# A second pair of block products taken one level further apart in two of sixteen groups

## Chip, core and metric

The kernel runs on one core of one Trainium2 chip. The metric is the device time of one execution in microseconds (us). The engines are named as in the profile: PE (TensorE matmuls), PEld (its weight loads), DVE (VectorE), ACT (ScalarE), POOL (GpSimd, which here only issues DMAs) and SP (SyncE, which issues the stores).

## What is computed

```python
m, k, n = 4096, 4096, 4096          # a, b: standard normal, float32
def reference(a, b):
    x = np.matmul(a, b)
    return 0.5 * x * (1 + np.tanh(np.sqrt(2 / np.pi) * (x + 0.044715 * x**3)))
```

The output is float32. The operands are rounded to float16 when they are loaded, and the sums are kept in float32.

## The kernel before

**Seven products instead of eight.** A and B are cut into quadrants of 2048 x 2048, and the four quadrants of the output are put together from seven products of sums of quadrants (Strassen's method). `PRODUCTS` lists them as (name, chain, A operand, B operand); `("11", "12", -1)` means A11 - A12, and a bare `"22"` means the quadrant itself:

```python
    ("M3", "Y", "11", ("12", "22", 1)),
    ("M5", "X", ("11", "12", -1), "22"),
    ("M7", "X", ("12", "22", -1), ("21", "22", 1)),
    ("M1", "X", ("11", "22", -1), ("11", "22", -1)),
    ("M4", "X", "22", ("21", "11", 1)),
    ("M2", "Y", ("22", "21", -1), "11"),
    ("M6", "Y", ("21", "11", -1), ("11", "12", 1)),
```

**Groups and steps.** The output quadrants are worked off in 16 groups, 0 to 15. A group is a block of 512 rows and 512 columns in each quadrant: (mb, nb), with mb changing every four groups. A group does its seven products in the order above (the last group has the order `LAST`). A product has a depth of 2048 and takes 4 steps (q = 0 to 3) of 16 matmuls, each 128 x 128 weights times 128 x 512. Products of one chain, X or Y, add up in the same four PSUM banks; `bank` (L390) gives a group four banks for X and four for Y, which swap roles from group to group. `settle` takes a product out of PSUM when its last step has run through bank i, by ACT copies (L513), DVE additions (L549), the gelu on ACT (L540) and the store by SP (L543).

**Split products.** In the groups of `SPLIT_GROUPS` (11, 13, 14, 15) the pair M3 and M5 goes one level further: each is itself done as seven products, "1" to "7", on quarters of its operands. `PAIR` is their order: "2", "1", "3" of M3, the same of M5, then "4", "5" of both, then "7", "6" of both. A small step is 16 matmuls of 128 x 256 (L483); in "2" the first matmul of each of two banks is 512 wide, to clear the whole bank. The parts are joined in PSUM and in a tile `join` by ACT copies (L501, L506) and DVE additions (L498). If an A operand is a sum of quadrants, the sum is first built in two tiles `aD` (four DVE instructions), and five of the seven small products take a further sum of its quarters.

**Where operands come from.** In the groups 0 to 5 the B sums are built on DVE (L365) and stored to DRAM, in units `k_M...` of 1 MB (two for each product). From group 6 on B is no longer in SBUF: the units are fetched (L760, `fetch`, a POOL DMA) into a ring of eight tiles of 1 MB. For a split pair the seven units `k_split` are fetched, two small operands in each. They are built in the groups 6, 7, 9 and 10 (the `maker` of each nb) by `make_split`: the quarters are added by DVE (L763, into one of three buffers `bS`) and stored by SP (L337); the two raw quarters, "2" and "5", of each product are copied out of the ring tile into `k_split` by SP alone.

**The order is planned by hand.** `steps` is the list of all steps of PE. Before the kernel is written out, a loop over the groups from 6 on hangs tasks on step numbers: an operand sum of A two steps ahead of its use (`AHEAD`), or six for split steps (`SPLIT_AHEAD`); a fetch at most twelve steps ahead (`FETCH_AHEAD`) and not before its ring tile is free; `ring_place` gives out the eight tiles in turn. `before` holds what comes from outside this plan: loads of A into the two `stage` tiles (L206, POOL), their transposition (L181, DVE) and the row checks (L228, ACT). The tasks give each engine's queue its order; an engine then runs each instruction as soon as its own waits are over, also ahead of the step that it is hung on. All queues are strictly in order, POOL's and SP's too, so one waiting fetch holds back all that are behind it.

A second path, `general_path`, is in the program for inputs whose range the checks reject; it does not run here.

Of the kernel before, what the change touches and what calls it, by code (L numbers as in the profile page):

```python
# [7 lines left out]
F32 = mybir.dt.float32  # L8
F16 = mybir.dt.float16
# [29 lines left out]

LAST = [PRODUCTS[k] for k in (0, 1, 3, 4, 5, 6, 2)]  # L40
NP = len(PRODUCTS)
QPH = 4
# [12 lines left out]

PAIR = [(s, p) for ps in ("213", "45", "76") for s in (0, 1) for p in ps]
SPLIT_AHEAD = 6
FETCH_AHEAD = 12
SPLIT_GROUPS = (11, 13, 14, 15)
CHECK_GROUP = 9  # L60
# [60 lines left out]
def half_path(  # L121
# [199 lines left out]
    def product(gi, s):  # L321
        return (LAST if gi == len(groups) - 1 else PRODUCTS)[s]

# [64 lines left out]
    post = {}  # L388

    def bank(gi, chain, i):  # L390
        par = (gi + (chain == "Y")) % 2
        t = psum_pool.tile([P, NC], F32, name=f"acc{chain}", tag=f"bank{par}{i}")
        banks[chain, i] = t
        return t
# [58 lines left out]
    def multiply(gi, s, q):  # L453
        name, chain = product(gi, s)[:2]
        first = q == 0 and name in ("M3", "M5")
        sa, sb = sums.pop((gi, s, q))
        for i in range(RT):
            acc = bank(gi, chain, i) if first else banks[chain, i]
            products(acc, sa, sb, i, first, q == QPH - 1)
            if q == QPH - 1:  # L460
                settle(gi, name, i)
# [7 lines left out]
    def multiply_split(gi, s, p):  # L469
# [6 lines left out]
        for r in range(RT // 2):  # L476
# [12 lines left out]
            if p in "76":  # L489
                settle(gi, name, i)  # L490
        if p in "24":
            joins[chain, p] = pool.tile([P, NC], F32, name="join", tag="x1", bufs=RT)
        for r in range(RT // 2):
            def join(p):
                return joins[chain, p][:, r * NC // 2 : (r + 1) * NC // 2]

            def joined(out, x, y, op):
                nc.vector.tensor_tensor(out=out, in0=x, in1=y, op=op)  # L498

            if p == "2":  # L500
                nc.scalar.copy(out=join("2"), in_=region(chain, "21", r))  # L501
            elif p == "3":
                joined(join("2"), region(chain, "12", r), join("2"), ALU.subtract)
                joined(join("2"), region(chain, "11", r), join("2"), ALU.add)
            elif p == "4":
                nc.scalar.copy(out=region(chain, "22", r), in_=join("2"))  # L506
                joined(join("4"), region(chain, "21", r), join("2"), ALU.add)
            elif p == "5":
                joined(region(chain, "11", r), join("4"), region(chain, "12", r), ALU.subtract)

# [40 lines left out]
    def settle(gi, name, i):  # L551

        X, Y = banks.get(("X", i)), banks.get(("Y", i))
        end = gi == len(groups) - 1
        if name == "M5":
            if end:
# [26 lines left out]
        elif name == "M6":  # L583
# [3 lines left out]
            waiting.append((gi, i, 1, 1, y, y))  # L587


    steps = [(0, -1, n) for n in range(N_PLAIN)]  # L590
    steps += [(0, s, q) for s in range(NP) for q in range(QPH // 2, QPH)]
    for gi in range(1, len(groups)):
        if gi in SPLIT_GROUPS:
            steps += [(gi, s, p) for s, p in PAIR]
        else:
            steps += [(gi, s, q) for s in (0, 1) for q in range(QPH)]
        steps += [(gi, s, q) for s in range(2, NP) for q in range(QPH)]
    position = {step: n for n, step in enumerate(steps)}
# [3 lines left out]
    def step_number(gi, s, q):  # L602
        gi, s = gi + s // NP, s % NP
        return position.get((gi, s, q), first_step[gi] + s * len(SPLIT) + 2 * q)

# [66 lines left out]
    def stage_block(mb, turns, turned=True):  # L672
        def do(n, fn, *args):
            before.setdefault(n, []).append((fn, args))

        for (quad, c), n in zip(chunks, turns):
            do(n - 6, load, (load_a, (mb, quad, c)))
            if turned:
                do(n, turn_a, mb, quad, c)
            for x in range(3):  # L680
                do(n + 1 + x, weigh_rows, mb, quad, c, list(range(NX))[x * 6 : (x + 1) * 6])
            if c == CH - 1 and quad in ("12", "21"):
                do(n + 4, weigh_half, mb, int(quad[0]) - 1)
# [52 lines left out]
    )}  # L736
    n_ring = 0
    tasks = {}
# [4 lines left out]

    def ring_place(need, ahead):

        nonlocal n_ring
        x = n_ring % len(ring)
        n_ring += 1
        n = max(ring_end[x] + 1, need - ahead)
        assert n <= need, (steps[need], steps[n])  # L750
        return x, n

# [5 lines left out]
    def fetch(key, x):  # L758
        t = split_tiles[key] = ring_tile(x, "bK")
        nc.gpsimd.dma_start(out=t, in_=kept_unit(*key[1:])[:, :])  # L760

# [10 lines left out]

    def blocks_a(gi, o):

        if isinstance(o, str):
            return [a_tiles[groups[gi][0], o, c] for c in range(CH)]
        return [
            split_tiles["d", gi, c].rearrange("p (jj m) -> p jj m", jj=NJ // 2) for c in range(CH)
        ]

    def open_block(gi, c, x):
        split_tiles["d", gi, c] = ring_tile(x, "aD")

    def block_sum(gi, o, q):

        w = 4 * NC
        t = split_tiles["d", gi, q // 2][:, (q % 2) * w : (q % 2 + 1) * w]
        mb = groups[gi][0]
        take(t, o[2], part(a_tiles, mb, o[0], q), part(a_tiles, mb, o[1], q))

    def operand_a(gi, s, q, tag):
        o = product(gi, s)[2]
        t = pool.tile([P, 4 * NC], F16, name="aS", tag=tag, bufs=AHEAD + 1)
        if q in SPLIT:
            y, z, op = SPLIT[q][1]
            blocks = blocks_a(gi, o)
            t = t.rearrange("p (jj m) -> p jj m", jj=NJ // 2)
# [6 lines left out]
    def operands(gi, s, q):  # L804
# [5 lines left out]
        if q in SPLIT:  # L810
            if sa is None:
                sa = quarter_a(blocks_a(gi, oa), SPLIT[q][1])
            k = PAIR.index((s, q))
            sb = split_tiles[gi, nb, "split", k // 2][:, (k % 2) * w : (k % 2 + 1) * w]
        else:
# [4 lines left out]

    def make_split(gi, s, p):

        nb = groups[gi][1]
        blocks = [split_tiles[gi, nb, product(gi, s)[0], c] for c in range(CH)]
        o = SPLIT[p][2]
        if isinstance(o, str):
            t = quarter_b(blocks, o)
        else:
            t = pool.tile([P, 4 * NC], F16, name="bS", tag="bS", bufs=AHEAD + 1)
            take(  # L830
                t.rearrange("p (x y) -> p x y", x=NJ)[:, :, :],
                o[2], quarter_b(blocks, o[0]), quarter_b(blocks, o[1]),
            )
            t = t[:, :]
        k = PAIR.index((s, p))
        keep_operand((nb, "split", k // 2), k % 2, t)

# [4 lines left out]
    n_a = 0  # L842
    last_a = 0
    for gi in range(N_RAW, len(groups)):
        n0, nb = first_step[gi], groups[gi][1]
        split = (gi, 0, "1") in position
        made = gi == maker[nb]
        mine = [n for n in range(n0, first_step.get(gi + 1, len(steps)))]
        ready = position[gi - 1, NP - 1, 2] if groups[gi][0] != groups[gi - 1][0] else 0
        units, block_users = {}, []  # L850
        makes = [
            (position[gi, s + 1 + k // QPH, k % QPH], s, p)
            for s in (0, 1) for k, p in enumerate("1346725")
        ] if made else []
        for n in mine:
            _, s, q = steps[n]
            name, _, oa, ob = product(gi, s)

            block = q in SPLIT and not isinstance(oa, str)
            if block and q == PAIR[0][1]:  # L860
                places = [ring_place(n, SPLIT_AHEAD) for c in range(CH)]
                e = max(ready, last_a, *(e for _, e in places))
                for c, (x, _) in enumerate(places):
                    task(e, open_block, gi, c, x)
                for qq in range(QPH):
                    task(e, block_sum, gi, oa, qq)
                last_a = e
            o = SPLIT[q][1] if q in SPLIT else oa
            e = n
            if not isinstance(o, str):  # L870
                tag = "aS" if made or n_a % 2 else "bS"
                n_a += 1
                e = max(n - (SPLIT_AHEAD if q in SPLIT else AHEAD), ready, last_a, free[tag][-AHEAD - 1] + 1)
                assert e <= n, steps[n]
# [3 lines left out]
            if block:  # L878
                block_users.append(max(e, n if isinstance(o, str) else 0))
                for x, _ in places:  # L880
                    ring_end[x] = max(block_users)
            task(n, operands, gi, s, q)

            key = (gi, nb, "split", PAIR.index((s, q)) // 2) if q in SPLIT else (gi, nb, name, q // 2)
            if key not in units:
                units[key], e = ring_place(n, FETCH_AHEAD)
                task(e, fetch, key, units[key])
            ring_end[units[key]] = max(n, *(e for e, s1, _ in makes if s1 == s)) if s < 2 and made else n
        for e, s, p in makes:
            task(e, make_split, gi, s, p)  # L890
            if not isinstance(SPLIT[p][2], str):
                free["bS"].append(e)

# [63 lines left out]
```

## Time and profile before

| | |
|---|---|
| Median of the runs | 1577.27 us (1575.31 to 1580.08, 4 runs) |
| Profiled execution: its own time / its span | 1577.12 us / 1575.5 us |
| Granted PE clock, mean | 0.997 |
| PE busy | 1560.0 us, 99% of the span |
| DVE busy | 1034.4 us, 66% |
| ACT busy | 656.5 us, 42% |
| DMA moved | 399.96 MB, mean 254 GB/s |

The span runs from the first to the last instruction on the core; the execution's own time has 1.6 us more around it. In the timeline lines the columns are: start in us, duration of the merged run of instructions in us, engine, line, operation, out<-in tiles, form, count; a bracket at the end says how long the engine was idle before and what ended the wait. In the waits, the columns are who waited, for whom, and the total in us, the number of times and the longest in us. A matmul's row is longer than its share of the stream, since matmuls are pipelined; the pace is read from the starts.

### The profile page before, as it was taken

To read this page: it belongs to the slowest core of one execution; us is meant where nothing else is said; L and a number is where in the kernel's file an instruction comes from. 1 tells how busy PE (TensorE), PEld (TensorE's weight loads), DVE (VectorE), ACT (ScalarE), POOL (GpSimd) and SP (SyncE) were. 2 spreads that over 40 slices of the span, in tenths; PEclk is the share of its full clock that TensorE was granted. 3 is DMA by queue.
4 is the path that set the end of the run, shared out by engine and by line. 5 is a ranking of instruction groups with operands and counts; after the bars stand their busy time and mean duration, and the time that the engine had idled before them with its cause. 6 is when DMAs were issued, how large, how long until landed. Compare 5 with 4: busy or idle time off the path is not lost. (4 is left out here: it accounts for less than half of the span.)

```text
span 1575.5 us, 21111 instructions
## 1 busy us (share of the span) xinstructions
PE 1560.0 (99%) x7630; PEld 747.8 (47%) x7630; DVE 1034.4 (66%) x1189; ACT 656.5 (42%) x1638; POOL 367.2 (23%) x652
## 2 busy tenths in 40 slices
PE   9999999999999999999999999999999999999998
PEld 4444444444444444444444444445644456474643
DVE  1697887969888886746555654466664574673853
ACT  1036444338874641212566344554456632121111
POOL 7763433341124300010222102101222101010100
PEclk9999999999999999999999999999999999999999
DMA  9999999994799985888999889999999667483752
GB/s 178 198 222 291 261 306 270 287 204 76 203 228 296 296 317 229 304 311 237 332 267 281 265 241 335 300 319 294 322 308 259 211 227 299 148 338 132 273 206 82
DMA packets 226336, 399.96 MB, mean 254 GB/s; under 512 B 17328, under 2 KB 156592, under 8 KB 204720
## 3 DMA queue, kind: packets, MB, share of 16 engines
q0 software_dynamic: 152704, 243.31, 64.8%
q1 hardware_dynamic: 73520, 155.22, 26.8%
q8 instruction: 62, 1.02, 0.3%
q14 instruction: 50, 0.41, 0.1%
HBM read 327.16 MB, written 155.19 MB: 306 GB/s over the span
## 5 line engine op out<-in xcount | busy, mean ns | idle before, releaser
L401 PEld LDWEIGHTS <-aS 128*128 128x128 f16 x4704 | 460.6, 98 | 562.0 <-issue 9.4
L401 PE MATMUL accX<-bK,aS 128*128 128x512 f16 x1664 | 360.9, 379 | 0.0
L763 DVE TENSOR_TENSOR aS<-aT 128x2048 f16<-128x2048 f16 x204 | 241.2, 1218 | 85.5 <-PE accX L401 57.8
L401 PE MATMUL accY<-bK,aS 128*128 128x512 f16 x1280 | 279.7, 381 | 2.4 <-DMA bK<-k_M 2.3
L401 PEld LDWEIGHTS <-aT 128*128 128x128 f16 x1728 | 169.6, 98 | 207.8 <-issue 5.1
L540 ACT ACTIVATE y<-y 128x512 f32<-128x512 f32 x192 | 119.0, 629 | 284.9 <-DVE y L549 284.7
L228 ACT ACTIVATE scrap<-stage 128x256 bf16<-128x256 f16 x512 | 212.8, 416 | 53.5 <-DMA stage<-in_a_dram 38.6
L206 POOL DMA_DIRECT2D bR<-in_b_dram x320 | 173.1, 544 | 209.0 <-DMA bR<-in_b_dram 113.2
L760 POOL DMA_DIRECT2D bK<-k_M x124 | 67.7, 547 | 516.3 <-DVE aS L763 102.4
L206 POOL DMA_DIRECT2D stage<-in_a_dram x176 | 111.5, 641 | 224.9 <-ACT scrap L228 177.1
L365 DVE TENSOR_TENSOR aS<-aT 128x2048 f16<-128x2048 f16 (+1 forms) x112 | 134.0, 1201 | 34.8 <-PE accX L401 25.9
L401 PE MATMUL accX<-bS,aS 128*128 128x512 f16 x704 | 153.2, 379 | 1.3 <-ACT x L513 0.7
L513 ACT COPY x<-accX 128x512 f32<-128x512 f32 x128 | 74.5, 585 | 178.5 <-PE accX L401 172.4
L365 DVE TENSOR_TENSOR bS<-bR 128x2048 f16<-128x2048 f16 x110 | 133.8, 1219 | 16.4 <-PE accX L401 12.1
L250 ACT ACTIVATE square<-bR 128x1024 bf16<-128x1024 f16 x120 | 122.9, 1049 | 48.5 <-DVE energy L549 48.3
L401 PE MATMUL accX<-bK,aT 128*128 128x512 f16 x640 | 139.8, 379 | 0.0
L181 DVE STREAM_TRANSPOSE aT<-stage 128x2048 uint32<-128x2048 uint32 (+1 forms) x37 | 74.6, 2018 | 74.2 <-DMA stage<-in_a_dram 73.3
L513 ACT COPY m<-accX 128x512 f32<-128x512 f32 x60 | 34.5, 580 | 195.7 <-PE accX L401 175.9
L549 DVE TENSOR_TENSOR x<-x,x 128x512 f32<-128x512 f32 x64 | 43.8, 684 | 82.2 <-ACT x L513 82.2
L228 ACT ACTIVATION_READ_ACCUMULATOR scrap<-stage 128x1 f32 x512 | 95.6, 187 | 0.0
L549 DVE TENSOR_TENSOR energy<-energy,square 128x1024 bf16<-128x1024 bf16 x120 | 82.1, 684 | 9.6 <-ACT square L250 7.9
L401 PE MATMUL accY<-bK,aT 128*128 128x512 f16 x384 | 83.9, 379 | 0.0
(63 smaller groups left out, 1127.1 us busy)
## 6 DMA issues: line engine op xcount, KB each, us to landing
bK<-k_M POOLq DMA_DIRECT2D x124, 1024.0 KB, 10.4
out_dram<-y SPq DMA_DIRECT2D x256, 256.0 KB, 6.7
bR<-in_b_dram POOLq DMA_DIRECT2D x320, 128.0 KB, 7.5
k_M<-bS SPq DMA_DIRECT2D x80, 512.0 KB, 6.5
stage<-in_a_dram POOLq DMA_DIRECT2D x144, 256.0 KB, 10.3
bK<-k_split POOLq DMA_DIRECT2D x28, 1024.0 KB, 6.6
k_split<-bS SPq DMA_DIRECT2D x40, 512.0 KB, 4.9
k_M<-bR SPq DMA_DIRECT2D x16, 1024.0 KB, 12.3
```

What stands on the lines that cost most here:

```text
L181: nc.vector.transpose(dst[:, :, x, :], src[:, :, x, :])
L206: nc.gpsimd.dma_start(out=dst, in_=src)
L228: nc.scalar.activation(weighed[mb, quad, c][:, :RUN], s[:, x, :], ACT.Square, accum_out=weighed[mb, ih][:, k, x : x + 1])
L250: nc.scalar.activation(t[:, :], src, ACT.Square)
L365: nc.vector.tensor_tensor(out=x, in0=y, in1=z, op=ALU.add if o[2] > 0 else ALU.subtract)
L401: nc.tensor.matmul(acc[:, :], sa[:, j // 2, i * P : (i + 1) * P, j % 2], sb[:, j, :], start=start and j == 0, stop=stop and j == 3, skip_g ...
L513: nc.scalar.copy(out=t[:, :], in_=src[:, :])
L540: nc.scalar.activation(y[:, :], src[:, :], ACT.Gelu_apprx_tanh)
L549: nc.vector.tensor_tensor(out=o[:, :], in0=x[:, :], in1=y[:, :], op=op)
L760: nc.gpsimd.dma_start(out=t, in_=kept_unit(*key[1:])[:, :])
L763: nc.vector.tensor_tensor(out=t, in0=y, in1=z, op=ALU.add if op > 0 else ALU.subtract)
```

## The change

In the groups 13 and 14 the pair M2 and M1 is split into small products as well, next to M3 and M5 (`SPLITS`). For that these two groups take the products in the order `FRESH`: M3, M5, M7, M2, M1, M4, M6. M2 and M1 each begin a chain anew, M2 in Y, with M4 after it, and M1 in X, with M6 after it. `settle_fresh` takes the parts out: M3, M7, M2 and M1 are copied by ACT to SBUF, and M2 and M1 are added there to the two running tiles x1 and x7; M4 gives two output blocks, M6 one. Such a group hands its two sets of banks on unswapped (`x_banks`).

The small operands are now made for both pairs in each of the groups 6, 7, 9 and 10: 20 sums in place of 10 sums and 4 raw copies, at the places that `MAKES` lists. Raw quarters are no longer written to `k_split`: `fetch` reads them from the unit of the whole, as a separate DMA of 512 KB in pieces of 512 bytes, beside another of 512 KB for the unit's other half. The ring gives out the tile that comes free first, not the next in turn. There is one `join` tile for each chain, taken from the two buffers `m5`.

```diff
+FRESH = [PRODUCTS[k] for k in (0, 1, 2)] + [
+    ("M2", "Y", ("21", "22", -1), "11"), PRODUCTS[3], ("M4", "Y", "22", ("21", "11", 1)),
+    ("M6", "X", ("21", "11", -1), ("11", "12", 1)),
+]
...
+MAKES = (("M3", (1, 0)), ("M5", (2, 1)), ("M1", (4, 0)), ("M2", (5, 3)))
+M3_M5, M2_M1 = 0, 3
...
-SPLIT_GROUPS = (11, 13, 14, 15)
+SPLITS = {M3_M5: (11, 13, 14, 15), M2_M1: (13, 14)}
...
-        par = (gi + (chain == "Y")) % 2
+        par = (x_banks[gi] + (chain == "Y")) % 2
...
+    def settle_fresh(gi, name, i, X, Y):
+        if name == "M3":
+            post["x1", i] = keep("x1", Y, RT)
+        elif name == "M2":
+            m2, x1, x7 = keep("m5", Y, 2), post["x1", i], post["x7", i]
+            tt(x1, x1, m2, ALU.subtract)
+            tt(x7, x7, m2, ALU.subtract)
+        elif name == "M1":
+            m1, x7 = keep("m5", X, 2), post["x7", i]
+            tt(x7, x7, m1, ALU.add)
+        elif name == "M4":
+            emit(gi, i, 1, 0, new_y(), Y)
+            y = new_y()
+            tt(y, Y, post.pop(("x7", i)), ALU.add)
+            flush()
+            waiting.append((gi, i, 0, 0, y, y))
...
-        x = n_ring % len(ring)
+        x = min(ring_end, key=ring_end.get)
...
     def fetch(key, x):
         t = split_tiles[key] = ring_tile(x, "bK")
...
+        (half, name, kw), = raw
+        unit = kept_unit(key[1], name, int(kw[0]) - 1)
+        for x in range(2):
+            dst = t[:, x * w : (x + 1) * w]
+            if x != half:
+                nc.gpsimd.dma_start(out=dst, in_=kept_unit(*key[1:])[:, x * w : (x + 1) * w])
+            else:
+                nc.gpsimd.dma_start(
+                    out=dst.rearrange("p (x y) -> p x y", x=NJ), in_=quarter_b({int(kw[0]) - 1: unit}, kw)
+                )
...
-        if isinstance(o, str):
-            t = quarter_b(blocks, o)
-        else:
-            t = pool.tile([P, 4 * NC], F16, name="bS", tag="bS", bufs=AHEAD + 1)
```

## The prediction

> **What bounds the kernel now.** I read the busy times first, then what PE waited for, then PE's timeline.
>
> ```profile
> PE 1560.0 (99%) x7630; PEld 747.8 (47%) x7630; DVE 1034.4 (66%) x1189; ACT 656.5 (42%) x1638; POOL 367.2 (23%) x652
> ```
>
> PE is busy all the time at a granted clock of 0.997, so the time is the sum of PE's steps plus its waits, and the waits are few:
>
> ```profile
> PE accY L401 <- DVE bS L365: 2.6, 1, 2.6
> PE accY L401 <- DMA bK<-k_M: 2.3, 1, 2.3
> PE accY L401 <- DVE y L549: 1.8, 2, 1.4
> ```
>
> The first and third lie before 560 us, in code that the change leaves alone. The second stands at 971 us, in group 9, which the change touches. From group 10 to the end of the stream PE has no wait at all, so what PE does there is the time. What a product costs is read from starts in PE's timeline of group 13's end and group 14's split pair:
>
> ```profile
> 1340.36 13.98 PE L401 MATMUL accX<-bK,aT 128*128 128x512 f16 x64
> 1354.17 27.79 PE L401 MATMUL accY<-bK,aS 128*128 128x512 f16 x128
> 1381.80 3.87 PE L483 MATMUL accY<-bK,aS 128*128 128x512 f16 x32
> 1385.50 1.91 PE L483 MATMUL accY<-bK,aT 128*128 128x256 f16 x16
> 1387.25 3.87 PE L483 MATMUL accX<-bK,aS 128*128 128x512 f16 x32
> ...
> 1392.70 1.91 PE L483 MATMUL accY<-bK,aT 128*128 128x256 f16 x16
> ...
> 1399.69 3.66 PE L483 MATMUL accY<-bK,aS 128*128 128x256 f16 x32
> ...
> 1406.68 3.62 PE L401 MATMUL accX<-bK,aS 128*128 128x512 f16 x16
> ```
>
> A whole product: 1354.17 - 1340.36 = 13.81 us (64 matmuls, 216 ns each). A split pair: 1406.68 - 1381.80 = 24.88 us, against 27.62 for two whole products.
>
> **PE's part.** Two pairs, M2 and M1 of groups 13 and 14, are exchanged: 2 x (27.62 - 24.88) = 5.5 us less. The built order of the changed kernel bears this out: 192 matmuls more, 2 x 2 x (112 - 64). A small matmul takes (1387.25 - 1385.50)/16 = 109 ns, and its weight load, 98 ns on average in the groups, hides behind it. The Trainium skill speaks against this: "TensorE: Matmul & The Clock Gate", section "Back-to-back issue gap", has the spacing set by load and matmul together, 81 ns at N=128 where the bare formula gives 56; were those 25 ns to fall on each of the 448 small matmuls, 11.2 us would be added and the change would lose. The row shows 109 ns with every load in place, so the sum goes by the row.
>
> **The stall at 971 us.** POOL's and PE's timelines show its cause:
>
> ```profile
> 947.43 0.60 POOL L760 DMA_DIRECT2D bK<-k_M  x1
> 960.28 0.56 POOL L760 DMA_DIRECT2D bK<-k_M  x1 [12.25 <-DMA k_split<-bK]
> ```
>
> ```profile
> 971.21 19.11 PE L401 MATMUL accY<-bK,aS 128*128 128x512 f16 x80 [2.33 <-DMA bK<-k_M]
> ```
>
> The fetch for M2 sat in POOL's queue until the copy of a raw quarter out of its ring tile had landed; such copies took up to 20.9 us in that stretch. The change has no such copies. Counted in the steps of its plan, M2's first unit is fetched 10 steps of 3.45 us ahead instead of 5 (34.5 against 17.3 us), and the least lead of a maker group is 24.2 us, for M4. The fetch that stalled took 10.9 us. I count the 2.3 us as gone. What is late next there: the ten further sums and stores of each maker group (below).
>
> **DVE in groups 13 and 14.** Each gets 10 more sums: 18 for M2 and M1 in place of 8. Twelve joins and four writes back to PSUM are added as well; settling stays at 24 additions (before: M5, M4, M2 and M6 4 each, and 8 after M1; then M2 8, M5, M1, M4 and M6 4 each). The windows:
>
> ```profile
> 1313.00:1382.00 69.00, 69.00 (x321) 31.26 (x320) 39.33 (x44) 12.83 (x23) 4.31 (x8) 1.00 0.53 202
> 1382.00:1407.00 25.00, 25.00 (x226) 22.01 (x225) 17.11 (x28) 6.59 (x15) 4.83 (x9) 1.00 0.90 334
> ```
>
> (columns: stretch, length, busy time and count of PE, PEld, DVE, ACT, POOL, clock, DMA share, GB/s). After the pair DVE has 39.3 of 69 us; 10 sums at 1.15 us (the pace in the next rows: 6 in 6.89) and 16 joins at 0.42 add 18.2, so 57.5 of 66.3. It fits, but the order decides:
>
> ```profile
> 1406.36 1.22 DVE L763 TENSOR_TENSOR aS<-aT 128x2048 f16<-128x2048 f16 x1
> 1407.61 1.29 DVE L549 TENSOR_TENSOR y<-accY,m 128x512 f32<-128x512 f32 x2
> 1408.81 6.89 DVE L763 TENSOR_TENSOR aS<-aT 128x2048 f16<-128x2048 f16 x6
> ```
>
> M5 ends at 1406.68 and DVE is free of its settling at 1408.81. It then runs sums ahead of PE, six in a row here. In the new queue follow: 2 sums of M7, 4 for M2's aD, 1 for M2's "2" = 7, done at 1416.9; M2 starts at M7's end, 1406.68 + 13.81 = 1420.5: 3.6 us to spare. Then 1 more for M2, 4 for M1's aD, 1 for M1's "2" = 13 in all, done at 1423.7, needed 5.45 us after 1420.5: 2.2 to spare. The tightest is the join before M2's "7", which PE reaches 17.89 us into the pair (1399.69 - 1381.80), at 1438.4. DVE has 15 sums queued (to 1426.0), 4 joins, 3 sums, 4 joins of M1 that wait for PE until 1431.4, a sum, 2 joins, a sum, 2 joins: 1437.0, so 1.4 us to spare. I count nothing. M2's and M1's later additions have M4's 13.8 us to hide in. M4 asks for eight `y` buffers of five within 3 us; stores landed after 2.0 to 6.2 us in the window 1350 to 1382, most after 2.0, while the sums queued behind on DVE are due 6.9 us after M4's end: nothing. `join` and `m5` share two buffers: M1's last join is done 18.5 us into a pair (1399.89 + 0.43 - 1381.80), the copy that takes its buffer comes at 19.6: nothing.
>
> **Fetches.** In the second pair four ring tiles hold A blocks, so four are left for seven units. Units 3 to 6 are issued when PE leaves their tiles and needed 10.9, 10.7, 10.5 and 10.5 us later; units 3 and 4 have a raw quarter. A whole fetch takes 5.1 us alone (window 1330 to 1362) and 6.3 to 11.0 in a crowded pair (1382 to 1402). No outputs are issued during the second pair. POOL's 24 further DMAs take 0.54 us each, and it waits 3 us or more for tiles between fetches. The price of a fetch in 512-byte pieces isn't in the trace; nearest are these:
>
> ```profile
> bK<-k_split POOLq DMA_DIRECT2D x28, 1024.0 KB, 6.6
> k_split<-bS SPq DMA_DIRECT2D x40, 512.0 KB, 4.9
> k_split<-bK SPq DMA_DIRECT2D x16, 512.0 KB, 10.5
> ```
>
> Below: as a whole fetch, 5.1 us, no stall. Above: as the worst copy of a quarter, 20.9 us, 10 us late in each group. I take the former: the slow copies lay in a stretch at a DMA share of 1.03, here it is 0.53 outside the first pairs, and this is a read.
>
> **Maker groups and group 11.** 40 more sums of 1.15 us and, net, 24 more stores of 512 KB fall into groups 6, 7, 9 and 10, where DVE is busy 51 to 59 of 97 us: 11.5 us more each fits. A sum that waits for a buffer waits for a store three steps (10.4 us) before it; those took 4.9, and a late A sum has two steps of cover. Dear is only the boundary from 10 to 11: the last two sums of M2 go ahead of M6's settling, which ended at 1098.59 + 2.48 = 1101.07, while M5's first matmul on those banks came at 1102.66. 2 x 1.15 us push it to 1103.4 at most, and the third of the four banks, which PE needs first, to 1102.8. Three units of group 11's first pair also lose lead (28.1, 24.7 and 21.3 us by the plan, then 14.3, 10.9 and 14.4). I take 0.5 us, with 0 and 3 as bounds.
>
> **Sum.** 1577.1 - 5.5 - 2.3 + 0.5 = 1569.8. The profiled execution (1577.12) stands 0.15 us under the median, so I leave it so. About 0.2% (3.2 us) is what a measurement of this kernel can tell from no change.
>
> **Rivals.**
> (a) The 2.3 us stay, or the makers' traffic (DMA share about 1.0 in these groups) costs as much at another place: 1572.1, to 1574 with group 11's upper bound. For it: fetches issued from 960 to 1000 landed after 7.8 to 17.5 us. Against: the longer leads.
> (b) DVE binds the second pair. In the first pair DVE lost 4.1 us to waits in the pair (2.70, 0.29, 0.22, 0.45, 0.45). All of it on the tightest join: 4.1 - 1.4 = 2.7 us a group, 1575.2. Against: it has a backlog there, so most of these waits fall into work.
> (c) Slower: raw quarters land late in the second pair. Every microsecond over 10.9 is paid by PE in each group, once. At 14.6 us the whole gain of 7.3 is gone; at 20.9 the time is 1569.8 + 20 = 1589.8. Against it stands the low DMA share.
> The Trainium skill puts the cost of small pieces lower: "DMA: Bandwidth & Descriptors", section "Why small descriptors are slow (HBM only)", gives about 3 cycles per packet, 27% at 256 bytes, hence an estimate of some 16% at 512; by that (c) would not happen, and no run here shows it.
> (d) The extra sums hold up the queues of the maker groups by several us each, 1574 to 1580.
>
> **Numbers.** Forecast 0.58; (a) 0.17; (b) 0.08; (c) 0.07; (d) 0.10. Range: the forecast less the spread of the runs below the median (1577.27 - 1575.31 = 2.0) and the 0.5 us of group 11, 1567.3, up to (b), 1575.2. Faster by over 0.2% (under 1574.1): forecast, (a), and part of (b) and (d), 0.80. Within 0.2%: the rest of (b) and most of (d), 0.12. Slower: (c) and a little, 0.08.
>
> **What would show it.** Right: no PE wait for `bK` or `aS` from 1290 us on; second pairs of 24.9 us; the gap at 971 gone; M5 of group 11 at most 0.5 us late. Wrong: PE waiting for `bK<-k_M` in M2's "4" (c), for DVE `accY` before "7" (b), for `aS` in groups 6 to 10 (d).

## The result, and the profile after

The changed kernel takes 1574.66 us in the median (1571.86 to 1577.92, 41 runs), the kernel before 1576.93 us (62 runs): a ratio of 0.9983, 95% interval 0.9978 to 0.9989. That is 2.3 us less where 7.3 were forecast. The profiled execution took 1574.24 us, its span is 1572.7 us, the granted clock 0.998. The busy times:

```profile
PE 1554.0 (99%) x7822; PEld 766.3 (49%) x7822; DVE 1112.1 (71%) x1281; ACT 670.2 (43%) x1670; POOL 392.3 (25%) x682
```

What PE waited for:

```profile
PE accX L418 <- ACT x L529: 4.6, 2, 4.0
PE accY L418 <- DVE y L565: 2.2, 2, 1.8
...
PE accX L500 <- DVE y L565: 1.2, 1, 1.2
```

The 2.3 us for `bK<-k_M` are gone. The longest wait is a new one, of 4.0 us for ACT. PE's timeline puts it, and the one of 1.2 us, in group 11:

```profile
1098.77 3.87 PE L500 MATMUL accX<-bK,aS 128*128 128x512 f16 x32 [1.20 <-DVE y L565]
...
1118.19 13.98 PE L418 MATMUL accX<-bK,aS 128*128 128x512 f16 x64
1136.14 16.84 PE L418 MATMUL accX<-bK,aS 128*128 128x512 f16 x64 [3.98 <-ACT x L529]
```

The 64 matmuls of M7 have a row of 13.98 us, the 64 of M1 behind the wait one of 16.84 us: 2.86 us more for the same work. The windows around it give the reason (stretch, length, then busy time and count of PE, PEld, DVE, ACT, POOL, then clock, DMA share, GB/s):

```profile
1132.00:1136.20 4.20, 0.23 (x2) 0.16 (x2) 3.73 (x3) 3.63 (x14) 1.11 (x2) 0.87 1.03 429
1136.20:1142.20 6.00, 6.00 (x15) 2.06 (x15) 3.09 (x3) 5.75 (x21) 0.53 (x1) 0.52 1.32 240
1142.20:1152.00 9.80, 9.80 (x47) 4.45 (x46) 3.23 (x3) 1.77 (x5) 3.17 (x5) 1.00 1.14 328
```

For 6 us after the wait the granted clock is 0.52; then it is whole again. A wait of 4 us cost nearly 7. The kernel before shows the same behind its wait at 971 us:

```profile
968.90:971.20 2.30, 0.00 (x0) 0.00 (x0) 2.13 (x3) 2.19 (x8) 1.72 (x3) 1.00 1.00 394
971.20:975.20 4.00, 3.99 (x12) 1.58 (x12) 0.17 (x1) 3.78 (x16) 0.95 (x2) 0.61 1.03 426
```

The second pairs run as planned, again from PE's timeline of the changed kernel:

```profile
1329.64 3.87 PE L500 MATMUL accY<-bK,aS 128*128 128x512 f16 x32
...
1354.52 13.98 PE L418 MATMUL accY<-bK,aT 128*128 128x512 f16 x64
...
1420.84 3.87 PE L500 MATMUL accY<-bK,aS 128*128 128x512 f16 x32
...
1438.74 3.66 PE L500 MATMUL accY<-bK,aS 128*128 128x256 f16 x32
...
1445.72 13.98 PE L418 MATMUL accY<-bK,aT 128*128 128x512 f16 x64
```

From "2" to the product after the pair it is 24.88 us in both groups, and no row has a wait.

The ledger of the two profiled executions: -5.5 us for the pairs; -4.0 at 971 us (the wait of 2.33, and 29.47 against 27.79 us for the 128 matmuls behind it); +8.0 in group 11 (1.20 + 3.98 + 2.86); -0.9 before 400 us, in code that is the same in both. The sum is -2.4; the spans differ by 2.8, of which 0.4 lie behind the start of PE's last product. Only the first three terms have to do with the change.

**How group 11 comes to wait.** POOL's timeline of the changed kernel:

```profile
1085.50 0.54 POOL L818 DMA_DIRECT2D bK<-k_split  x1 [19.28 <-PE accY L418]
1094.94 0.53 POOL L825 DMA_DIRECT2D bK<-k_split  x1 [8.90 <-DVE bS L832]
1095.46 0.91 POOL L827 DMA_DIRECT2D bK<-k_M  x1
1096.36 0.54 POOL L825 DMA_DIRECT2D bK<-k_split  x1
1096.89 0.91 POOL L827 DMA_DIRECT2D bK<-k_M  x1
1097.79 1.06 POOL L818 DMA_DIRECT2D bK<-k_split  x2
...
1110.79 1.97 POOL L217 DMA_DIRECT2D stage<-in_a_dram  x3
```

And of the kernel before, the fetches for the same pair and the same load:

```profile
1076.95 0.54 POOL L760 DMA_DIRECT2D bK<-k_split  x1 [9.80 <-PE accY L401]
1083.86 0.54 POOL L760 DMA_DIRECT2D bK<-k_split  x1 [6.37 <-PE accY L401]
...
1114.37 2.58 POOL L206 DMA_DIRECT2D stage<-in_a_dram  x4
```

In group 10 the maker's sums for M2 come last, one in each of the last five steps from (5, 3) on, and the plan keeps both ring tiles with M2's two units until the last of them. PE is done with these tiles before that, so the sums alone hold them. The next fetch for group 11 therefore stands 19.28 us in POOL's queue, until PE leaves a tile of M6 at 1085.50. The one behind it waits 8.90 us more for DVE to be done with the last sum, and then four units go out within 4 us; before the change they went out one by one, 6.9 us apart at first, from 1076.95 to 1101.38. Behind them comes the load of A's new row block into `stage`, a megabyte in four DMAs. DVE's timeline shows when it was there:

```profile
1132.47 2.31 DVE L192 STREAM_TRANSPOSE aT<-stage 128x2048 uint32<-128x2048 uint32 x1 [9.79 <-DMA stage<-in_a_dram]
1134.70 4.59 DVE L832 TENSOR_TENSOR aS<-aT 128x2048 f16<-128x2048 f16 x4
```

And ACT's, in which this row check stands ahead of the copies that free M7's banks for M1:

```profile
1132.41 0.42 ACT L239 ACTIVATE scrap<-stage 128x256 bf16<-128x256 f16 x1 [11.33 <-DMA stage<-in_a_dram]
```

From the first load's issue to the transposition it took 21.7 us (1132.47 - 1110.79); before the change, 14.3 (1128.63 - 1114.37):

```profile
1128.63 2.31 DVE L181 STREAM_TRANSPOSE aT<-stage 128x2048 uint32<-128x2048 uint32 x1 [2.05 <-DMA stage<-in_a_dram]
```

The load is issued hardly later than before: its first DMA 7.4 us ahead of M7's first matmul (1118.19 - 1110.79), before the change 7.7. It lands late: the DMAs of this load and the next took 17.2 us from issue to landing in the median, before the change 14.4. The stores of the sums are no large part of what it has to share the DMA queues with: between 1094 and 1133 us 13.15 MB were moved, and of M2's five stores only the last, 0.5 MB, was issued then.

### The profile page after: what moved, and what is told of

It reads as the page before. It is cut to its first block, busy times and chain, and to the rows that moved or that the text cites. A ratio compares the mean times of both kernels' runs of the same rounds, so it can differ in the third digit from the quotient of the medians.

```text
span 1572.7 us, 21821 instructions
## 1 busy us (share of the span) xinstructions
PE 1554.0 (99%) x7822; PEld 766.3 (49%) x7822; DVE 1112.1 (71%) x1281; ACT 670.2 (43%) x1670; POOL 392.3 (25%) x682
## 5 line engine op out<-in xcount | busy, mean ns | idle before, releaser
L418 PEld LDWEIGHTS <-aS 128*128 128x128 f16 x4448 | 435.7, 98 | 535.8 <-issue 10.0
L832 DVE TENSOR_TENSOR aS<-aT 128x2048 f16<-128x2048 f16 x188 | 223.3, 1218 | 58.5 <-PE accX L418 47.4
L418 PE MATMUL accY<-bK,aS 128*128 128x512 f16 x1024 | 222.3, 379 | 0.0
L818 POOL DMA_DIRECT2D bK<-k_M x116 | 62.7, 542 | 452.0 <-PE accX L418 126.7
L529 ACT COPY x<-accX 128x512 f32<-128x512 f32 x120 | 69.6, 586 | 158.2 <-PE accX L418 152.2
L529 ACT COPY m<-accX 128x512 f32<-128x512 f32 x68 | 39.3, 582 | 187.7 <-PE accX L418 175.1
L832 DVE TENSOR_TENSOR bS<-bK 128x2048 f16<-128x2048 f16 x80 | 97.0, 1218 | 26.7 <-DMA k_split<-bS 26.7
L418 PE MATMUL accY<-bK,aT 128*128 128x512 f16 x512 | 111.8, 379 | 0.0
L418 PE MATMUL accX<-bK,aT 128*128 128x512 f16 x512 | 111.8, 379 | 0.0
L500 PEld LDWEIGHTS <-aS 128*128 128x128 f16 x960 | 93.9, 98 | 16.1 <-issue 1.4
```

Of the source, the lines that this page charges most:

```text
L418: nc.tensor.matmul(acc[:, :], sa[:, j // 2, i * P : (i + 1) * P, j % 2], sb[:, j, :], start=start and j == 0, stop=stop and j == 3, skip_g ...
L500: nc.tensor.matmul(banks[chain, i][:, :] if wide else out, sa[:, j // 2, r * P : (r + 1) * P, j % 2], sb[:, : NC] if wide else sb[:, j * N ...
L529: nc.scalar.copy(out=t[:, :], in_=src[:, :])
L832: nc.vector.tensor_tensor(out=t, in0=y, in1=z, op=ALU.add if op > 0 else ALU.subtract)
```

## The experiments

The theory, A in the expectations: the M2 sums at the end of group 10 cause all of group 11's loss, by the held tiles, the bunched fetches and the late load. Its point: M2 and M1 are split in groups 13 and 14 alone, so the sums made in groups 6 and 10, for the other two nb, are read by nobody. The rivals: the 512-byte pieces of the raw quarters slow the DMA queues down (B); the load is simply issued too close to its use (C); the second pair itself costs (D); the added sums and stores cost by their traffic, wherever they lie (E). All medians stand against the kernel before on the same chip.

**1. Only the sums that are read** (in the loop over `MAKES`; all products stay):

```diff
+                if not any(groups[g][1] == nb for g in SPLITS[s0]):
+                    continue
```

> The changed kernel, but the small sums of M2 and M1 are made only where groups 13 and 14 use them, in the makers 7 and 9; groups 6 and 10 no longer make theirs, which nobody reads. Theory A (tiles held): the loss of the changed kernel lies at the boundary from group 10 to 11, where the last two unused sums keep a ring tile and DVE, so that three fetches go out together, the next load of A lands late, ACT waits for it with the copy of M7 behind it, and PE waits 4.0 us and then runs slowly for 2.9 us more. Then both PE waits of group 11 (1.2 and 4.0 us) go, with the slow stretch: 1.2 + 4.0 + 2.9 = 8.1 us, so about 1566.6. Rival B (small pieces): the reads in 512-byte pieces fill the DMA queue; then the 4.0 us stay, and only the 1.2 us of DVE go: about 1573.5. Rival C (short lead): the load of A is hung too close to its use in group 11; the stall becomes smaller but stays: about 1570.

Measured: 1565.18 us (before 1576.3), ratio 0.9932, 0.9919 to 0.9946. POOL's timeline of this kernel has the fetches apart again, and PE's has no wait in group 11:

```profile
1074.26 0.54 POOL L818 DMA_DIRECT2D bK<-k_split  x1 [9.25 <-PE accY L418]
1081.16 0.53 POOL L825 DMA_DIRECT2D bK<-k_split  x1 [6.37 <-PE accY L418]
...
1088.07 0.54 POOL L825 DMA_DIRECT2D bK<-k_split  x1 [5.48 <-PE accY L418]
...
1094.98 0.54 POOL L818 DMA_DIRECT2D bK<-k_split  x1 [5.47 <-PE accY L418]
```

```profile
1119.39 27.79 PE L418 MATMUL accX<-bK,aS 128*128 128x512 f16 x128
```

M7 and M1 are one run of 128 matmuls. This is the fastest version found, 0.68% (10.7 us, interval 8.5 to 12.8) below the kernel before, about what the pairs (5.5) and the stall at 971 (4.0) are worth together. It leaves out two makers' sums at once, so it does not yet tell the place from the traffic. It speaks against B, which had 1573.5, and C, which had 1570: the slowest run took 1568.16 us.

**2. The load of A earlier** (all sums kept):

```diff
-            do(max(n - LOAD_AHEAD, free_at.pop(0)), load, (load_a, (mb, quad, c)))
+            ahead = LOAD_AHEAD + 4 * (mb == NMB - 1 and quad == "11")
+            do(max(n - ahead, free_at.pop(0)), load, (load_a, (mb, quad, c)))
```

> The changed kernel, with the first two loads of A for the last block of rows hung ten steps ahead of their use in place of six; the rest as it is. Theory A: the queue is backed up from the three late fetches on, and these loads now go ahead of two or three of the fetches in POOL's queue; the copy of M7 is no longer late (6.9 us less), but the 1.2 us at M5 stay and fetches of the first pair may come late instead: 1567.8 to 1572. Rival C (short lead): the whole 6.9 us go and nothing takes their place: 1567.8. Rival B (small pieces): the queue is just as full, the stall only moves: about 1574.

Measured: 1569.13 us (before 1576.3), 0.9955, 0.9941 to 0.9968. M1's wait is gone; M5's is 3.16 us in its profile, with a slow stretch behind it (5.54 us for a row that is 3.87 elsewhere):

```profile
1103.49 5.54 PE L500 MATMUL accX<-bK,aS 128*128 128x512 f16 x32 [3.16 <-DVE y L565]
```

So the late load is what M1 waits for. Moving it gives back four to five of the eight us by the medians, 3.2 by the two profiles (8.0 against 3.16 + 1.67); the fetches are still held, the second for 10.86 us.

**3. The raw quarters as whole pieces.** The raw quarter is read as one stretch of 4 KB in each partition. These are other columns, so that the split groups compute something else; the bytes and the number of DMAs stay.

```diff
-                    out=dst.rearrange("p (x y) -> p x y", x=NJ), in_=quarter_b({int(kw[0]) - 1: unit}, kw)
+                    out=dst, in_=unit[:, (int(kw[1]) - 1) * w : int(kw[1]) * w]
```

> The changed kernel, but each raw quarter is read as one stretch of 4 KB per partition from the same unit, not as eight pieces of 512 bytes: as many bytes, of other columns, so the outputs of the split groups are not the reference's. Rival B (small pieces): the backlog in group 11 goes, and with it 6.9 us: about 1568. Theory A and rival C: the pieces cost little, the waits of group 11 stay within 1 us: 1573.5 to 1574.7.

Measured: 1574.18 us (before 1576.3), 0.9992, 0.9983 to 1.0001; the changed kernel's ratio is 0.9983. Waits of 0.77 and 4.79 us remain in group 11, together no shorter than with the small pieces (5.56 against 5.18 us). B falls.

**4. No second pair, and none of its sums** (M2 and M1 stay whole and the order of products stays the old one everywhere; raw quarters are still read from the whole's units, and the ring keeps its new rule):

```diff
-SPLITS = {M3_M5: (11, 13, 14, 15), M2_M1: (13, 14)}
+SPLITS = {M3_M5: (11, 13, 14, 15), M2_M1: ()}
```

together with the edit of 1.

> The changed kernel without the split of M2 and M1 and without their sums: what is left is the reading of raw quarters from the whole's units, the ring that gives out the first free tile, the new places of the sums of M3 and M5, and one join tile. Against the kernel before it lacks the copies of raw quarters. Theory A: the stall of 2.3 us in group 9 and the slow 1.7 us after it go, nothing is added: 1576.9 - 4.0 = 1572.9, and 5.5 us above the first kernel of this set, which has the second pair. Rival B: the stall of group 11 is here as well: about 1578 or more.

Measured: 1572.92 us (before 1576.3), 0.9977, 0.9968 to 0.9986. No wait at 971 us nor in group 11: without the second pair, what is left of the change (raw quarters read from the whole's units, the new rule of the ring, the new places of the sums) is a gain by itself. Which of these gives it was not taken apart.

**5. The sums alone**: the edit of `SPLITS` in 4 without that of 1. All twenty sums are made in each maker group, and nobody reads M2's and M1's.

> The changed kernel without the split of M2 and M1, but with all their sums still made and stored in groups 6, 7, 9 and 10. Theory A (tiles held): the loss comes with the sums, not with the pair that reads them: 1572.9 (the version without pair and sums) + 8.1 = 1581.0, slower than the kernel before. Rival D (the pair itself costs): the sums are hidden and the time stays at 1572.9.

Measured: 1581.11 us (before 1577.26), 1.0027, 1.0014 to 1.0039. Against 4 the sums cost 0.50%, 7.9 us, and all of it is in sight in PE's timeline of the profiled execution, which at 1582.86 us lies 1.75 above the median:

```profile
1100.97 3.87 PE L500 MATMUL accX<-bK,aS 128*128 128x512 f16 x32 [2.63 <-DVE y L565]
...
1139.04 16.32 PE L418 MATMUL accX<-bK,aS 128*128 128x512 f16 x64 [4.67 <-ACT x L529]
```

2.63 + 4.67 + (16.32 - 13.98) = 9.6 us. The pairs are unsplit here, so D falls. And without their gain the change would have made the kernel slower, although the stall at 971 us is gone here too.

**6. Both of 1 and 2.**

> The version that makes only the sums that are read, with the first two loads of A for the last block of rows hung ten steps ahead in place of six. Theory A: that version has no wait left in group 11, so nothing is to be had: 1565.2, within 1 us. Rival C (short lead): the short lead still costs in some executions; up to 2 us less.

Measured: 1567.31 us (before 1577.26), 0.9942, 0.9923 to 0.9962. That is 2.1 us above 1, where within 1 us was expected, but the two intervals overlap, and there is no wait in group 11 in either. With the tiles free in time the earlier load brings nothing.

**7. No M2 and M1 sums in group 6** (ten sums and their stores less, in another maker):

```diff
+                if gi == 6 and s0 == M2_M1:
+                    continue
```

> The changed kernel without group 6's unused sums of M2 and M1; group 10's unused ones are still made. Theory A: only group 10 stands ahead of a group that fetches a split pair, so nothing changes: 1574.7. Rival E (traffic): the 10 stores of 512 KB and 10 sums cost wherever they are; half of the 8 to 9 us goes: about 1570.

Measured: 1575.49 us (before 1577.26), 0.9994, 0.9982 to 1.0006. Waits of 1.26 and 3.09 us remain in group 11. The traffic of such sums, elsewhere, costs nothing that can be measured. In its profile no fetch for group 11 waits for DVE: POOL waits for PE up to 1094.71 us, and four units still go out, up to 1098.42. So what bunches them is the tiles that the plan keeps back up to the boundary, not a late sum on DVE.

**8. Only M2's five sums of group 10 left out:**

```diff
+                if gi == 10 and name == "M2":
+                    continue
```

> The changed kernel without the five sums of M2 in group 10, those that are made last before group 11; M1's five of group 10 and all of group 6 stay. Theory A: these five alone hold the ring tile and DVE, so both waits of group 11 go, with the slow stretch: 1574.7 - 8.1 = 1566.6. Rival E (traffic): five of twenty unused sums are a quarter: about 1572.5.

Measured: 1566.29 us (before 1577.26), 0.994, 0.992 to 0.996, and no wait in group 11; M7 and M1 are one run again:

```profile
1115.93 27.79 PE L418 MATMUL accX<-bK,aS 128*128 128x512 f16 x128
```

Five sums of 80 are all of the loss that can be measured: with 7 this settles which ones.

**9. The first row checks one step later** on ACT:

```diff
-                do(n + 1 + x, weigh_rows, mb, quad, c, list(range(NX))[x * 6 : (x + 1) * 6])
+                late = mb == NMB - 1 and quad == "11" and c == 0
+                do(n + 1 + x + late, weigh_rows, mb, quad, c, list(range(NX))[x * 6 : (x + 1) * 6])
```

> The changed kernel; of the last block of rows, the first chunk's three pieces of row checks on ACT are each hung one step later, so that M7's four copies stand ahead of the second piece, and only the first piece can still hold them up. Theory A: the late load holds PE only by way of ACT's queue, with the row checks that wait for it ahead of the copies of M7. Hung one step later, the first piece still stands just ahead of these copies (its step is the last of M7), so by A the wait at M1 stays, less the 1.6 us that the second piece took where it stood ahead: from 1574.7 to 1570. If the copies came before all pieces, 1567.8. Rival F (the copies are late for another reason, or PE waits for the load itself): no change, 1574.7.

Measured: 1574.49 us (before 1576.4), 0.9991, 0.9982 to 1.0. A miss for theory A, and the expectation also described the edit wrongly: all the checks of that chunk, the first too, now stand behind M7's copies, for which it had 1567.8. The number is that of rival F. ACT's timeline shows that the copies became punctual, PE's that it waited as long as ever, for DVE now:

```profile
1130.44 0.58 ACT L529 COPY x<-accX 128x512 f32<-128x512 f32 x1 [8.54 <-PE accX L418]
```

```profile
1137.04 13.28 PE L418 MATMUL accX<-bK,aS 128*128 128x512 f16 x49 [4.04 <-DVE aS L833]
```

```profile
1133.56 2.31 DVE L192 STREAM_TRANSPOSE aT<-stage 128x2048 uint32<-128x2048 uint32 x1 [10.06 <-DMA stage<-in_a_dram]
```

The third fence is DVE's timeline of the same kernel: the transposition waits for the load and stands ahead of M1's A sums. The part of the theory that had the late load reach PE by way of ACT alone fell: it reaches PE through two queues at once, and the profile had named the one that came last.

**10. M2's sums earlier in the makers**, all of them made, five of them read by nobody as before:

```diff
-MAKES = (("M3", (1, 0)), ("M5", (2, 1)), ("M1", (4, 0)), ("M2", (5, 3)))
+MAKES = (("M3", (1, 0)), ("M5", (2, 1)), ("M1", (4, 0)), ("M2", (5, 1)))
```

> The changed kernel with all its sums, those that nobody reads too, but M2's five are hung two steps earlier in each maker group, right behind M1's. Theory A: M2's last tile comes free and DVE is rid of its sums 6.9 us earlier, before the boundary from group 10 to 11, so both waits of group 11 go, at the same traffic: 1566.6. Rival E (traffic): as many bytes and sums as before, 1574.7.

Measured: 1568.78 us (before 1576.4), 0.9957, 0.9944 to 0.9971, at the same traffic, so E falls. Two steps earlier, the same sums leave 0.20 us of wait in group 11. In exchange PE waits in group 6. PE's timeline, DVE's and the window behind the wait:

```profile
694.38 15.53 PE L418 MATMUL accY<-bK,aS 128*128 128x512 f16 x64 [2.51 <-DVE y L565]
```

```profile
691.37 1.23 DVE L832 TENSOR_TENSOR bS<-bK 128x2048 f16<-128x2048 f16 x1 [5.10 <-DMA k_split<-bS]
```

```profile
694.30:697.50 3.20, 3.12 (x8) 1.16 (x8) 3.20 (x6) 2.42 (x4) 0.00 (x0) 0.50 0.76 291
```

A sum waited 5.10 us for a store to give back its buffer, and M6's settling stood behind it: 2.51 us, and 1.55 more at half the clock. This wait is a price of the new place; the median lies 2.2 us above the 1566.6 that were expected.

How the load's lateness decides is seen by one measure across the kernels: from M7's first matmul to the transposition. M1 follows 3.5 to 3.7 us behind the transposition's start (1136.14 - 1132.47; 1137.04 - 1133.56), and is due 13.8 us after M7's start, so the transposition may begin up to some 10.1 us after it. The rows are all kernels in which the transposition waited for the load (all but 2 and 6).

| Kernel | first load to transposition | M7 to transposition | M1 waited |
|---|---|---|---|
| before | 14.3 | 6.5 | 0 |
| after | 21.7 | 14.3 | 3.98 |
| 3, whole pieces | 22.6 | 15.1 | 4.79 |
| 5, the sums alone | 22.4 | 15.0 | 4.67 |
| 7, without group 6's | 20.3 | 13.4 | 3.09 |
| 9, checks later | 21.9 | 14.6 | 4.04 (for DVE) |
| 1, needed sums | 16.0 | 7.0 | 0 |
| 4, no second pair | 19.1 | 10.1 | 0 |
| 8, without M2 of group 10 | 16.1 | 7.1 | 0 |
| 10, M2's sums earlier | 16.5 | 9.2 | 0 |

Where PE waited, what is over 10.1 is 3.3 to 5.0 us, within half a us of the wait. Kernel 4 is a warning: its fetches go out apart, as in 1, and its load still took 19.1 us. There is one profile of each kernel, and a load's time differs by some 3 us between two with the same fetches, so not all of the lateness need come from the bunching.

## Why the prediction was right or wrong

- **PE's part, 5.5 us:** right, 24.88 us twice. Small matmuls keep the pace that the row of before showed; the loss by weight loads that was weighed against it did not come.
- **The stall at 971 us:** right that it goes (gone in the changed kernel and in 4), but the term of 2.3 us was mis-sized: with the slow clock behind it, it was worth 4.0.
- **DVE in the second pair:** right. The tightest join was forecast for 1437.0, on a need at 1438.4; its row ends at 1436.84 and "7" starts at 1438.74. Rival (b) did not happen.
- **Fetches with raw quarters:** right. In the second pair of group 14 they landed 6.2 to 6.4 us after their issue, 3.5 us ahead of their use, and 3 shows that the small pieces cost nothing that can be measured. Rival (c) did not happen. POOL's further DMAs were 30 (682 against 652), not 24, and one in small pieces took 0.91 us to issue, not 0.54; PE did not feel it.
- **Maker groups and group 11, "I take 0.5 us, with 0 and 3 as bounds":** this is the step that failed. It cost 8.0 us in the profiled execution. The two sums ahead of M6's settling were seen, and make the smaller wait: 1.20 us, within the bounds, though over the half us that the prediction named as its sign of being right. That three units lose lead was seen too, and their leads were long enough: PE waited for no unit. Not seen was what units that go out together do to the load of A behind them in POOL's queue; its lead was not looked at. And the bounds were set for waits alone, without the clock behind them: 3.98 us became 6.84.
- **The rivals:** (d) was nearest in kind, since the extra sums do hold up a queue; but it had all maker groups lose, and 7, 8 and 10 show that it is one place. (a) had the traffic as cause, and 7 and 10 speak against it.

With the measured sizes the sum is 1577.1 - 5.5 - 4.0 + 8.0 = 1575.6, or 1574.7 with the 0.9 us of the early part, where the profiled execution took 1574.24. The error was in one term, larger than its upper bound, and a part of it was made up for by the second, too small on the other side. That the time still falls inside the stated range is luck: the range's upper end was drawn from rival (b), which did not happen.

That the five sums at that place are the cause is shown by 8, 10 and 7, and that PE waits at M1 for the load is shown by 2 and 9. The links between, from the kept tiles to the bunch and from the bunch to the slow load, are read from the timelines. How long POOL waited is not the measure: in 10 the first fetch was held for 18.02 us, but it went out 8.1 us ahead of group 11's first matmul (1096.94 - 1088.81), while in the changed kernel the bunch went out 3.0 us behind it (1094.94 - 1091.95).

Open: 2 removes M1's wait alone, but no edit removes M5's alone. And how much of the lateness is the bunching and how much the load's nearness to it, or chance, was not measured by itself.

## What to carry to other kernels

An operand that is read once more, or later, keeps its buffer longer: follow that buffer to the next transfer that wants it, and from there through every instruction behind it in the same queue, to transfers that have nothing to do with the change. When work is added at a boundary between stages, ask of each piece whether anyone reads it; here five unread sums of 80 took back most of the gain. In this kernel a wait of PE that is longer than about 2.3 us has to be priced at up to twice its length, as the next table shows.

## What was not expected of the hardware

After a wait PE's granted clock can fall to about half for some 3 to 6 us, at full load: 0.52 over 6.0 us above, 0.50 over 3.2 us in 10. All waits of PE over 1.7 us, and what the run of matmuls behind them lost against its usual row (the kernel in brackets):

| Wait, us | Lost behind it, us |
|---|---|
| fifteen from 1.75 to 2.24 (1.77 in after, 2.24 in 8) | 0 |
| 2.31 (1), 2.33 (before), 2.37 (5), 2.49 (2) | 1.7 |
| 2.51 (10) | 1.55 |
| 2.62 (before), 2.85 (4) | 1.65, 1.3 |
| 2.63 (5, at 1100.97) | 0 |
| 2.90 (7), 3.09 (7), 3.16 (2) | 1.7 |
| 3.98 (after), 4.04 (9) | 2.86, 2.5 |
| 4.67 (5), 4.79 (3) | 2.3, 2.9 |

The boundary is not sharp. In 5 the clock stayed whole behind 2.63 us, as the window shows:

```profile
1101.00:1104.00 3.00, 3.00 (x26) 2.50 (x26) 2.93 (x6) 2.37 (x6) 0.59 (x2) 1.00 0.96 277
```

The Trainium skill, "TensorE: Matmul & The Clock Gate", section "HAM oscillation — how this bites in real kernels", asks for no idle gaps of PE over about 3.4 us. The waits of 3.98 us and more agree; all but one of those from 2.31 to 3.16 us lost clock too, and there the measurement decides.
